# Another order of the hand-written step list behind the attention: row norms, weight halves, modulation rows and feed-forward heads

## Chip, cores, metric

The kernel runs on one core of one Trainium2 chip. The metric is the time of one execution on the device in microseconds (us). The core's engines work side by side, each through a queue of its own in order: PE (TensorE) multiplies and transposes, ACT (ScalarE) and DVE (VectorE) work elementwise and read the results of PE, POOL (GpSimd) works elementwise as well, SP (SyncE) starts most DMA transfers. An engine waits at an instruction until what it reads is written, and everything behind that instruction in its queue waits with it.

## The reference

Two layers of a diffusion backbone over 512 latent tokens and 256 context tokens of width 1024, batch 1. Layer 0 mixes tokens by windowed attention, layer 1 by a gMLP; behind each stands a SwiGLU FFN.

```python
for i in range(DEPTH):
    sh_ml, sc_ml, g_ml, sh_fl, sc_fl, g_fl = jnp.split(silu(c) @ ada_w[i] + ada_b[i], 6, axis=-1)
    h_l = modulate(rmsnorm(x, norm_g[i, 0]), sh_ml, sc_ml)          # h * (1 + scale) + shift
    if kind == 0:
        y_l, y_c = window_sink_mixer(h_l, h_c, ...)
    elif kind == 1:                                                 # gMLP
        z = gelu(h_l @ w_in + b_in)
        u, v = split(z)
        v = layernorm(v, ln_g, ln_b)                                # in chunks of 128 tokens
        y_l = (u * (einsum('gpq,bnqgc->bnpgc', w_s, v) + b_s)) @ w_o
    x = x + g_ml * rmsnorm(y_l, norm_g[i, 1])
    h = modulate(rmsnorm(x, norm_g[i, 2]), sh_fl, sc_fl)
    gate, up = jnp.split(h @ ffn_w_in[i], 2, axis=-1)
    x = x + g_fl * rmsnorm((silu(gate) * up) @ ffn_w_out[i], norm_g[i, 3])
```

## The kernel before

Products are computed in split precision: each float32 operand becomes a high half (`high`, L216, a cast on ACT, L217) and a low half (`low`, L219, a subtraction on DVE, L224), and each product is three matmuls: high by high, high by low, low by high (L273 to L275, L281). Weights come in units through a stream: `wfetch_u` starts the load of unit u on SP, `whigh_u_h` and `wlow_u_h` make the halves of its half h.

The 512 tokens are four row tiles of 128. Behind each mixer's and each FFN's last product, a `Chain` object for each tile t does what the lines of the reference between two products say. Its steps, with their engines, are: `square_y` (ACT), `gain_y` (DVE, L1150), `rstd_y` (DVE, then a power on POOL, L254), `add_x` (DVE, L1154), `square_x` (ACT), `gain_x` (POOL, L1166), `rstd_x` (DVE, POOL), `shift_x_z` (DVE, L1170) for the halves z, `turn_z` (four PE transposes, L1177), `turned_hi_z` (ACT) and `turned_lo_z` (DVE), which write the operand H of the next product. In the step list they are `c0square_y`, `c1turn_0` and so on; "#2" and "#3" mark the second and third use of a name. `c2merge` and `c3merge` add a part of the attention's out-projection that was computed earlier.

Four groups of steps are drawn into the change's reach:

- The last two units of the attention's out-projection (`work_2_t`, `work_3_t`: 12 matmuls of 512 columns each), made by `down`, with the four chains and the heads of FFN 0. A head is the first hidden tile's product for one row tile: `f0head_t_0` and `f0head_t_1` are 12 matmuls each, `f0head_t_2` is Silu on ACT (L1328), its product with the other half on DVE (L1329), and, for t over 0, the PE transposes (L1338) of tile t − 1 and their copy on DVE (L1339). Beside them stand the preparations of the FFN's later products, which are done in a fast-multiplication scheme with sums and differences of quarters: `f0first_half` (ACT), `f0sum_a_*` (DVE, L1378), `f0sum_high_*` and `f0sum_low_*` (the halves of these sums), `f0diff_2_*` (POOL, L1409), `f0part_high_*` and `f0part_low_*` (halves of weight quarters). The FFN's own products (L1449) come behind.
- The last units of FFN 0's second product (`work_9_t`, `work_10_t`), with the chains and the first two units of the gMLP's v (`<lambda>_t_n`).
- The gMLP: `v_part`, the layer norm of v (`v0add` to `v3bias`), `u_part`, `mixed_g` (L1882), and two modulation rows, each made from eight chunks (`m2fetch_chunk_k` on SP, `m2add_chunk_k` on DVE, L383), a fold of its halves by a DMA that POOL starts (`m2fold`, L397), and `m2mirror`, `m2stack`, `m2total`, `m2done`; `m4...` likewise.
- The gMLP's out-projection with the chains and the heads of FFN 1 (`f1...`), as in the first group.

What sets the order is one long text, `ORDER` (from L41): the names of all steps in the sequence in which they are to be issued. The code first collects steps with `at(time, step, ...)`, which makes a name and looks up its rank in that text; a step whose name isn't there goes behind all others by its planned time. `run_plan` then sorts what was collected and issues it:

```python
def run_plan():
    for _, _, key, step, args in sorted(plan, key=lambda e: e[:2]):
        step(*args)
    plan.clear()
```

So ranks count only among the steps of one `run_plan`. The attention has its own ones, and each of the four groups above is one. Where the `run_plan` stands in a `manual_schedule`, as for these groups, each engine's queue has the sequence of the text. The steps of the two FFNs between the groups aren't in the text and go by their planned times.

## Time and profile before

| | us |
|---|---|
| median of 3 runs | 1109.13 (1108.85 to 1111.06) |
| the profiled execution, its span from the first to the last instruction | 1108.2 |
| PE, gaps in the span | 19.9 |
| attention's out-projection, last units | about 250 to 300 of the span |
| FFN 0 | 300 to 593 |
| FFN 0's last units | 593 to 643 |
| gMLP | 643 to 717 |
| gMLP's out-projection | about 717 to 789 |
| FFN 1 | 789 to the end |

The profile is of one execution. The page gives each engine's busy time and its share of the span, the clock that TensorE was granted in 40 slices, and for each engine what ended its waits. The trace can be asked for windows (a row for each stretch: length, then busy time and, in brackets, count of instructions for PE, PE's weight loads, DVE, ACT and POOL, then the granted clock, the DMA share and GB/s), for a timeline of one engine (start, length, line, operation, what it writes and reads, and in square brackets the idle time before it and what ended that), and for a line's groups (count, then shortest, median and longest duration in ns). Neighbouring instructions of one kind share a row of the timeline ("x8"); the row's length reaches from the first start to the last end. Rows of DVE follow each other by less than their length, since the start of one overlaps the end of the one before.

### The profile page before, as it was taken

Reading aid. Unit: us, or ns where it says so; the run is one execution under the profiler, and the core shown is the slowest. Engines: PE = TensorE matmul, PEld = TensorE weight load, DVE = VectorE, ACT = ScalarE, POOL = GpSimd, SP = SyncE. Lnnn points to the kernel's source line nnn. Section 1 sums busy time; section 2 is a strip of 40 time slices with the busy share of each in tenths; the row PEclk is TensorE's granted clock in tenths of the full one; section 3 lists DMA queues with packets and bytes.
Section 4 is the critical chain, followed back from the end, with each engine's and each line's share of the span. In section 5 each row is a group of like instructions: output and inputs, shape, how many; then the busy total and the mean of one; then the engine's idle time right before and its main releaser. Section 6 shows DMA issues by size and latency. Waiting matters only on the chain.

```text
span 1108.2 us, 17883 instructions
## 1 busy us (share of the span) xinstructions
PE 1088.3 (98%) x6974; PEld 954.9 (86%) x6974; DVE 943.8 (85%) x1418; ACT 612.6 (55%) x1060; POOL 255.9 (23%) x276
## 2 busy tenths in 40 slices
PE   7999999999999999999999999999999999999997
...
PEclk9999999999999999999999999999999999999999
...
GB/s 366 266 182 86 136 96 115 77 135 113 109 143 172 224 159 185 171 141 330 225 122 128 68 323 241 205 194 77 70 133 124 132 152 126 126 222 319 158 40 76
DMA packets 48857, 179.15 MB, mean 162 GB/s; under 512 B 4859, under 2 KB 9211, under 8 KB 37637
## 3 DMA queue, kind: packets, MB, share of 16 engines
...
q14 instruction: 31, 0.25, 0.1%
...
## 4 chain that ended last, share of the span: by engine, by line
PE 64%; DVE 6%; POOL 2%; issue 2%; ACT 1%; DMA 1%; POOLq 0%; DVEq 0%; SPq 0%; ACTq 0%
PE f L1449 35%; PE y L1633 13%; PE y L1660 4%; PE v L281 4%; PE y L281 2%; PE u L1869 1%; PE u L1867 1%; PE u L1868 1%; POOL tmp L1166 1%; DVE w_lo L224 1%; DVE tmp L1170 1%; DVE x L1154 1%; PE mix L1882 1%; DMA w_raw<-in_w 1%; DVE a_sum L1378 1%
## 5 line engine op out<-in xcount | busy, mean ns | idle before, releaser
L1449 PE MATMUL f<-H,w_hi 128*128 128x256 f32 x960 | 178.6, 284 | 1.1 <-DVE fc L1460 0.5
L1449 PEld LDWEIGHTS f<-H,w_hi 128*128 128x128 f32 x960 | 149.7, 192 | 2.3 <-DVE fc L1460 1.4
L1449 PE MATMUL f<-H,w_lo 128*128 128x256 f32 x480 | 135.8, 283 | 0.0
L1633 PE MATMUL y<-w_hi,s 128*128 128x512 f32 x448 | 120.1, 389 | 0.0
L1449 PE MATMUL f<-S,w_hi 128*128 128x256 f32 x640 | 118.6, 283 | 0.0
L217 ACT CAST w_hi<-w_raw 128x1024 fp32r<-128x1024 f32 x90 | 94.5, 1053 | 39.9 <-PE y L1633 8.9
L217 ACT CAST w_hi<-T 128x1024 fp32r<-128x1024 f32 x80 | 83.7, 1047 | 52.4 <-PE f L1449 33.7
L1456 ACT COPY fc<-f 128x256 f32<-128x256 f32 x120 | 44.6, 372 | 105.8 <-PE f L1449 102.7
L224 DVE TENSOR_TENSOR w_lo<-w_raw,w_hi 128x1024 fp32r<-128x1024 f32 (+1 forms) x81 | 96.3, 1193 | 6.7 <-ACT w_hi L217 6.7
L1449 PEld LDWEIGHTS f<-S,w_hi 128*128 128x128 f32 x640 | 99.9, 192 | 0.0
L1633 PEld LDWEIGHTS y<-w_hi,s 128*128 128x128 f32 x448 | 84.1, 188 | 17.5
L224 DVE TENSOR_TENSOR w_lo<-T,w_hi 128x1024 fp32r<-128x1024 f32 x80 | 97.3, 1216 | 0.0
L1449 PEld LDWEIGHTS f<-H,w_lo 128*128 128x128 f32 x480 | 92.1, 192 | 0.0
L1449 PE MATMUL f<-S,w_lo 128*128 128x256 f32 x320 | 90.7, 284 | 0.5 <-DVE w_lo L224 0.5
L1621 POOL DMA_DIRECT2D t<-in_w x48 | 42.2, 929 | 186.5 <-PE y L1660 88.4
L383 DVE SCALAR_TENSOR_TENSOR acc<-ada_k,sc,acc 128x1024 f32<-128x1024 f32 x56 | 71.6, 1278 | 10.3 <-DMA ada_k<-in_ada 8.4
L397 POOL DMA_DIRECT2D acc<-acc x8 | 6.9, 866 | 314.2 <-DVE acc L383 310.4
L1633 PE MATMUL y<-w_lo,s 128*128 128x512 f32 x224 | 69.1, 390 | 0.6 <-DVE w_lo L224 0.6
L1449 PE MATMUL f<-H,x 128*128 128x256 f32 x480 | 64.3, 283 | 0.0
L932 POOL TENSOR_SCALAR p<-p,st 128x512 f32<-128x512 f32 (+1 forms) x64 | 53.4, 849 | 44.4 <-DVE st L928 11.7
L281 PE MATMUL y<-w_hi,st 128*128 128x512 f32 x224 | 62.3, 391 | 0.0
L1449 PEld LDWEIGHTS f<-S,w_lo 128*128 128x128 f32 x320 | 61.4, 192 | 0.9 <-DVE w_lo L224 0.9
...
## 6 DMA issues: line engine op xcount, KB each, us to landing
...
```

The costliest lines, as they stand in the source:

```text
L217: nc.scalar.copy(out=hi, in_=src)
L224: (eng or nc.vector).tensor_tensor(out=v(lo), in0=v(src), in1=v(hi).bitcast(F32), op=ALU.subtract)
L281: nc.tensor.matmul(dst, l, w[:, n * 512:(n + 1) * 512], start=first and i == 0, stop=last and i == 2)
L383: nc.vector.scalar_tensor_tensor(out=self.acc, in0=self.raws.pop(k), scalar=sc[:, k:k + 1], in1=self.acc, op0=ALU.mult, op1=ALU.add)
L932: nc.gpsimd.tensor_scalar(out=p, in0=p, scalar1=self.st[:, 12 + j:13 + j], scalar2=1.0, op0=ALU.mult, op1=ALU.mult)
L1154: nc.vector.scalar_tensor_tensor(out=xt, in0=self.tmp[:, c0:c1], scalar=self.r, in1=xt, op0=ALU.mult, op1=ALU.add)
L1166: nc.gpsimd.tensor_tensor(out=self.tmp[:, D:], in0=x[:, self.t, :], in1=self.nxt[0], op=ALU.mult)
L1449: nc.tensor.matmul(dst, l[:, w], r[:, k, :], start=first and k == 0 and j == 0, stop=k == 3 and j == 2, skip_group_check=True)
L1456: nc.scalar.copy(out=self.c[n][:, i * 256:(i + 1) * 256], in_=self.ps[n, 1 if i == 1 else 0])
L1621: nc.gpsimd.dma_start(out=self.tt[:, p * D + 512 * i:p * D + 512 * (i + 1)], in_=a["w"][F2[self.layer] + 1 + 2 * p + i][:, c:c + 512], acc ...
L1633: nc.tensor.matmul(self.bank7(i, j), st[:, c:c + P], w[:, z * 512:(z + 1) * 512], start=i == 1 and p == 0 and l == 0 and z == 0, stop=p == ...
L1660: nc.tensor.matmul(self.y[t][n], st[:, x + t * P:x + (t + 1) * P], parts[h][w][:, n * 512:(n + 1) * 512], start=v == 0 and h == 0 and i == ...
```

## The change

Only the text of `ORDER` is another one; no other line of the program differs. The new text has 1571 names instead of 1575; the four that are gone, `v0norm` to `v3norm`, name no step of the program. The attention's part has `q_first_0_1_6`, `m2fold`, `m2mirror`, `kv_7_5`, `m3stack` at other places relative to steps of other groups, and is else as before. The four groups behind it are ordered anew. Their lists, cut to the parts that the text below speaks of:

```diff
-rows_out_15 wo_part_3_1_3 wo_keep_3_1 store_15_1 store_15_0 work_2_0 whigh_10_0 whigh_10_1 m3stack_<lambda> wlow_10_0
-work_3_0 work_2_1 c0square_y wlow_10_1 work_3_1 c0gain_y c0rstd_y wfetch_11 c0add_x whigh_11_0 m3total_0_slot
-m3total_512_slot c0square_x c1square_y work_2_2 c0gain_x wlow_11_0 m3done_0 c0rstd_x c1gain_y m3done_512 work_3_2
-c1rstd_y c0shift_x_1 c0shift_x_0 c1add_x c0turn_1 c0turn_0 c1square_x c1gain_x c2merge work_2_3 c1rstd_x c2gain_y
-c0turned_hi_1 c2square_y c0turned_hi_0 c2rstd_y whigh_11_1 c0turned_lo_0 c1shift_x_0 c2add_x c1shift_x_1 c2gain_x
-work_3_3 table_Silu c2square_x c1turn_0 c3merge c2rstd_x c1turned_hi_0 c1turned_lo_0 f0first_half_1 f0head_0_0
-c1turn_1 wfetch_12 c3square_y c1turned_hi_1 c0turned_lo_1 wlow_11_1 c3rstd_y c3gain_y c2shift_x_0 f0diff_2_1
...
-c2turned_hi_0 c2turned_lo_0 f0sum_a_S2 f0part_low_2_0 c3shift_x_1 f0head_1_2 c3shift_x_0 f0sum_a_S4 f0head_2_0
-c3turn_0 f0first_half_0#2 c3turn_1 f0head_2_1 c3turned_hi_1 c3turned_hi_0 f0diff_2_3 c3turned_lo_0 c3turned_lo_1
-f0diff_2_2 f0diff_2_4 f0part_high_2_1 f0part_high_2_3 f0sum_a_S3#2 f0sum_a_S1 f0sum_a_S2#2 f0head_2_2 f0sum_a_S4#2
-f0sum_a_S1#2 f0head_3_0 f0sum_high_S4 f0sum_high_S2 f0sum_high_S1 f0head_3_1 wfetch_13 f0part_low_2_2 f0sum_low_S2
-f0head_3_2 f0sum_low_S1 f0sum_high_S3 f0part_low_2_1 f0sum_low_S4 f0part_low_2_3 f0sum_low_S3 work_9_1 whigh_43_0
-work_9_0 work_10_0 wlow_43_0 c0square_y#2 whigh_43_1 c0gain_y#2 wfetch_44 c0rstd_y#2 c0add_x#2 work_9_2 whigh_44_0
-<lambda>_1_2 work_10_1 wlow_43_1 wlow_44_0 <lambda>_2_2 c0square_x#2 c0rstd_x#2 c1square_y#2 c1gain_y#2 c0gain_x#2
-c1rstd_y#2 c0shift_x_0#2 wfetch_45 work_9_3 work_10_2 c2square_y#2 c0shift_x_1#2 c1add_x#2 c2gain_y#2 c1gain_x#2
...
-m2add_chunk_2 v0gelu m2fetch_chunk_5 wlow_47_1 v0mean m2add_chunk_3 v0var v_part_1_(3,) v0gain whigh_48_0
-m2add_chunk_4 m2fetch_chunk_6 v0norm m2add_chunk_5 m2fetch_chunk_7 v_part_2_(2,) v1add v0rstd whigh_48_1 m2add_chunk_6
-u_part_0_0 v1gelu m2add_chunk_7 v0bias v1mean m2fold#2 wlow_48_1 wfetch_49 v1gain m2fetch_gain#2 v_part_3_(3,)
...
-whigh_49_1 v2gelu u_part_1_1 v2mean v3add v2var wfetch_50 gelu_u_0_0 v3gelu gelu_u_0_1 v2gain m4add_chunk_1
-m4fetch_chunk_3 m4fetch_chunk_4 wlow_49_1 v2rstd m4add_chunk_2 v3mean wlow_49_0 v2norm v3var v2bias m4fetch_chunk_5
-wfetch_51 m2done_512#2 v3rstd m4add_chunk_3 m4add_chunk_4 m4fetch_chunk_6 u_part_2_1 v3norm whigh_50_0 v3gain
-u_part_2_0 m4add_chunk_5 m4fetch_chunk_7 gelu_u_1_0 gelu_u_1_1 v3bias m4add_chunk_6 m4add_chunk_7 m4fold#2
-m4fetch_gain#2 mixed_0 wlow_50_0 mixed_6 m4mirror#2 whigh_50_1 mixed_bias_0 mixed_1 whigh_51_0 mixed_u_0 mixed_bias_1
-mixed_5 mixed_3 mixed_u_1 mixed_4 mixed_bias_3 gelu_u_2_0 mixed_2 wlow_50_1 mixed_u_3 m4stack#2 u_part_3_0 whigh_51_1
...
-mixed_u_7 whigh_55_0 work_2_0#2 work_3_0#2 whigh_55_1 c0square_y#3 work_2_1#2 work_3_1#2 wfetch_56 whigh_56_0
-wlow_55_0 whigh_56_1 work_2_2#2 c1square_y#3 wlow_55_1 c0rstd_y#3 c0gain_y#3 c0add_x#3 m3total_0_slot#2
-m3total_512_slot#2 c0gain_x#3 c0square_x#3 wlow_56_0 c0rstd_x#3 m3done_512#2 m3done_0#2 work_3_2#2 c2square_y#3
-c1rstd_y#3 c1gain_y#3 c0shift_x_1#3 c0shift_x_0#3 c1add_x#3 c2gain_y#3 c0turn_1#3 c0turn_0#3 c1gain_x#3 c1square_x#3
-c1rstd_x#3 c2rstd_y#3 wfetch_57 c1shift_x_1#3 c0turned_hi_0#3 work_2_3#2 c1shift_x_0#3 c0turned_hi_1#3 c2add_x#3
...
-c3turned_hi_1#3 f1sum_a_S3 f1part_high_2_1 c2turned_lo_0#3 f1sum_a_S2 c2turned_lo_1#3 f1part_low_2_0 f1sum_a_S3#2
-f1sum_a_S1 c3turned_lo_0#3 f1first_half_1#2 f1sum_a_S2#2 f1sum_a_S4 f1head_1_2 f1head_2_0 f1head_2_1 f1sum_a_S4#2
-f1sum_high_S2 f1diff_2_4 f1sum_a_S1#2 c3turned_lo_1#3 f1part_high_2_3 f1head_2_2 f1sum_high_S4 f1head_3_0 f1sum_low_S4
-f1part_low_2_2 f1head_3_1 f1sum_high_S3 wfetch_58 f1sum_high_S1 f1head_3_2 f1sum_low_S1 f1part_low_2_1 f1sum_low_S2
-f1part_low_2_3 f1sum_low_S3
...
+wo_keep_3_1 store_15_1 store_15_0 m3stack_<lambda> work_2_0 whigh_10_0 whigh_10_1 wfetch_11 m3total_0_slot m3done_0
+m3total_512_slot wlow_10_0 work_3_0 c0square_y c0gain_y c0rstd_y c0add_x c0gain_x whigh_11_0 whigh_11_1 work_2_1
+m3done_512 wlow_10_1 work_3_1 c1gain_y c0square_x c0rstd_x c1square_y c1rstd_y wlow_11_0 c1add_x work_2_2 work_3_2
+c0shift_x_1 c0shift_x_0 c0turn_1 c1square_x c1rstd_x c2merge c1gain_x c2gain_y c2square_y c0turn_0 wlow_11_1
+c0turned_hi_0 work_2_3 c1shift_x_0 work_3_3 c2rstd_y c1shift_x_1 c0turned_lo_0 c0turned_hi_1 c1turn_1 c1turn_0
+c1turned_hi_0 c2add_x c2gain_x c3merge c2square_x f0head_0_0 c1turned_lo_0 c0turned_lo_1 c2rstd_x c2shift_x_1
...
+c3turn_0 f0diff_2_1 f0diff_2_3 f0diff_2_2 c2turned_hi_0 c2turned_lo_0 f0head_2_0 f0diff_2_4 c3shift_x_1 wfetch_13
+f0first_half_1 c3turn_1 f0sum_a_S2 c2turned_hi_1 c2turned_lo_1 f0sum_a_S1 f0first_half_1#2 f0head_2_1 f0part_high_2_0
+f0part_low_2_0 c3turned_hi_0 c3turned_lo_0 f0part_high_2_2 f0part_low_2_2 f0sum_a_S4 f0sum_a_S3#2 f0sum_a_S2#2
+f0sum_a_S4#2 f0part_high_2_1 f0sum_a_S1#2 c3turned_hi_1 f0part_high_2_3 f0sum_high_S4 f0head_1_2 f0sum_high_S1
+f0part_low_2_1 f0sum_high_S2 f0head_3_0 c3turned_lo_1 f0sum_low_S2 f0sum_low_S1 f0head_2_2 f0sum_low_S4 f0head_3_1
+f0sum_high_S3 f0head_3_2 f0part_low_2_3 f0sum_low_S3 table_Silu whigh_43_0 whigh_43_1 wlow_43_1 <lambda>_3_2 wfetch_44
+work_9_1 work_10_1 c1square_y#2 c1gain_y#2 c1rstd_y#2 c1add_x#2 c1gain_x#2 whigh_44_0 whigh_44_1 wlow_43_0 work_9_0
+work_10_0 c0gain_y#2 <lambda>_1_2 c0square_y#2 c0rstd_y#2 c0add_x#2 c0square_x#2 c1square_x#2 work_9_3 wlow_44_0
+c0gain_x#2 <lambda>_2_2 c0rstd_x#2 c0shift_x_1#2 work_9_2 work_10_2 c2square_y#2 c0turn_1#2 c0turned_hi_1#2
...
+v_part_1_(2,) v_part_1_(3,) row_in_1 m2add_chunk_2 m4fetch_chunk_0 m2fetch_chunk_5 v_part_2_(2,) m2fetch_chunk_6 v0add
+v_part_2_(3,) m2add_chunk_3 m2add_chunk_4 whigh_47_1 m2add_chunk_5 v_part_3_(2,) v_part_3_(3,) wlow_47_0 wfetch_48 v1add
+v1gelu m2fetch_chunk_7 v0gelu m2add_chunk_6 v0mean m4fetch_chunk_1 m2add_chunk_7 wlow_47_1 m2fold#2 row_in_2 v0var
...
+wlow_49_1 v3mean m4fetch_chunk_5 m4fetch_chunk_7 wlow_48_1 u_part_1_0 v2add v2gelu m4add_chunk_0 m4add_chunk_1 v3var
+m2total_0_slot wfetch_50 wlow_49_0 m4add_chunk_2 m4add_chunk_3 v2mean v2gain bias_in v3rstd v3gain v3bias ws_in
+gelu_u_0_0 m4fetch_gain#2 m4add_chunk_4 m4add_chunk_5 u_part_2_0 m4fetch_chunk_6 m4add_chunk_6 m4add_chunk_7 m4fold#2
+v2var v2rstd gelu_u_2_0 wfetch_51 whigh_50_0 whigh_50_1 m2total_512_slot v2bias wlow_50_0 u_part_2_1 gelu_u_2_1
+whigh_51_0 gelu_u_0_1 whigh_51_1 m2fetch_gain#2 m2done_512#2 wlow_51_1 u_part_1_1 mixed_1 m2done_0#2 mixed_2
+mixed_bias_1 mixed_u_1 wlow_50_1 mixed_5 mixed_3 gelu_u_1_0 mixed_0 gelu_u_1_1 mixed_4 mixed_bias_5 mixed_u_5
...
+mixed_u_6 gelu_u_3_1 mixed_7 mixed_bias_7 mixed_u_7 work_2_0#2 work_2_1#2 whigh_55_0 wlow_55_0 work_3_0#2 c0gain_y#3
+c0square_y#3 c0rstd_y#3 c0add_x#3 c0gain_x#3 work_3_1#2 c1gain_y#3 c1square_y#3 c1rstd_y#3 m3total_0_slot#2 c0square_x#3
+c0rstd_x#3 whigh_55_1 wlow_55_1 m3total_512_slot#2 wfetch_56 m3done_512#2 work_2_2#2 m3done_0#2 c0shift_x_0#3 work_3_2#2
+c0shift_x_1#3 whigh_56_0 c0turn_1#3 whigh_56_1 wfetch_57 c2square_y#3 c0turn_0#3 c1add_x#3 c1square_x#3 c1gain_x#3
+wlow_56_0 c2gain_y#3 work_2_3#2 c0turned_hi_0#3 c1rstd_x#3 c0turned_lo_0#3 f1first_half_1 c1shift_x_1#3 c2rstd_y#3
...
+f1sum_a_S3 f1sum_a_S2 f1diff_2_1 c3turn_0#3 c3shift_x_1#3 c2turned_hi_0#3 c2turned_lo_0#3 f1sum_a_S1 f1part_high_2_2
+c2turned_hi_1#3 c2turned_lo_1#3 f1first_half_0#2 f1diff_2_3 f1head_1_1 f1head_1_2 f1diff_2_2 c3turn_1#3 f1sum_a_S4
+c3turned_hi_1#3 c3turned_lo_1#3 f1diff_2_4 c3turned_hi_0#3 f1head_2_0 f1part_low_2_2 f1head_2_1 c3turned_lo_0#3
+f1sum_a_S3#2 f1sum_a_S2#2 f1part_high_2_3 f1sum_a_S1#2 f1sum_a_S4#2 f1part_low_2_3 f1sum_high_S1 f1sum_low_S1
+f1sum_high_S4 f1head_3_0 f1sum_low_S4 f1sum_high_S3 f1sum_low_S3 f1part_high_2_1 f1part_low_2_1 f1head_2_2 f1head_3_1
+f1sum_high_S2 f1sum_low_S2 f1head_3_2 table_Silu#2
```

Split into queues, the end of the first group reads on DVE and PE, before and after:

```
DVE before: ... f0head_1_2 c3shift_x_0 f0sum_a_S4 c3turned_lo_0 c3turned_lo_1 f0sum_a_S3#2 f0sum_a_S1 f0sum_a_S2#2 f0head_2_2
            f0sum_a_S4#2 f0sum_a_S1#2 f0part_low_2_2 f0sum_low_S2 f0head_3_2 f0sum_low_S1 ...
DVE after:  ... f0sum_a_S1 f0part_low_2_0 c3turned_lo_0 f0part_low_2_2 f0sum_a_S4 f0sum_a_S3#2 f0sum_a_S2#2 f0sum_a_S4#2
            f0sum_a_S1#2 f0head_1_2 f0part_low_2_1 c3turned_lo_1 f0sum_low_S2 f0sum_low_S1 f0head_2_2 f0sum_low_S4 f0head_3_2 ...
PE before:  ... f0head_1_1 f0head_1_2 f0head_2_0 c3turn_0 c3turn_1 f0head_2_1 f0head_2_2 f0head_3_0 f0head_3_1 f0head_3_2
PE after:   ... f0head_1_1 c3turn_0 f0head_2_0 c3turn_1 f0head_2_1 f0head_1_2 f0head_3_0 f0head_2_2 f0head_3_1 f0head_3_2
```

The end of the fourth group:

```
DVE before: ... f1sum_a_S1#2 c3turned_lo_1#3 f1head_2_2 f1sum_low_S4 f1part_low_2_2 f1head_3_2 f1sum_low_S1 f1part_low_2_1
            f1sum_low_S2 f1part_low_2_3 f1sum_low_S3
DVE after:  ... f1sum_a_S4#2 f1part_low_2_3 f1sum_low_S1 f1sum_low_S4 f1sum_low_S3 f1part_low_2_1 f1head_2_2 f1sum_low_S2 f1head_3_2
PE before:  ... f1head_2_1 f1head_2_2 f1head_3_0 f1head_3_1 f1head_3_2
PE after:   ... f1head_2_1 f1head_3_0 f1head_2_2 f1head_3_1 f1head_3_2
```

More of the change, by code (lines that the diff above doesn't have):

```diff
@@ L121 @@
[L121 to L124 removed]
+norm_in_4_1 turn_in_4_1 ada0_rows_out_3 modulated_low_1 modulate0_ctx_2 kv_1_2 kv_1_4 kv_1_5 turned_in_0_1 turned_in_4_1
@@ L155 @@
-c3turn_0 f0first_half_0#2 c3turn_1 f0head_2_1 c3turned_hi_1 c3turned_hi_0 f0diff_2_3 c3turned_lo_0 c3turned_lo_1
-f0diff_2_2 f0diff_2_4 f0part_high_2_1 f0part_high_2_3 f0sum_a_S3#2 f0sum_a_S1 f0sum_a_S2#2 f0head_2_2 f0sum_a_S4#2
-f0sum_a_S1#2 f0head_3_0 f0sum_high_S4 f0sum_high_S2 f0sum_high_S1 f0head_3_1 wfetch_13 f0part_low_2_2 f0sum_low_S2
-f0head_3_2 f0sum_low_S1 f0sum_high_S3 f0part_low_2_1 f0sum_low_S4 f0part_low_2_3 f0sum_low_S3 work_9_1 whigh_43_0
-work_9_0 work_10_0 wlow_43_0 c0square_y#2 whigh_43_1 c0gain_y#2 wfetch_44 c0rstd_y#2 c0add_x#2 work_9_2 whigh_44_0
@@ L195 @@
[L195 to L199 removed]
+rows_out_11 store_11_0 turned_12_2 bound_14_2 exp_14_2 bound_14_3 turn_12_3 wo_part_2_1_2 m3add_5 wo_part_2_1_3 exp_14_3
@@ L200 @@
+f1sum_high_S4 f1head_3_0 f1sum_low_S4 f1sum_high_S3 f1sum_low_S3 f1part_high_2_1 f1part_low_2_1 f1head_2_2 f1head_3_1
+f1sum_high_S2 f1sum_low_S2 f1head_3_2 table_Silu#2
 """.split()
```

233 lines of the change are left out of this document (115 added, 118 removed).

## Prediction

> **What bounds the kernel now.** I read the page first: its busy line, its clock row, then the waits of PE, then the windows of the stages whose order changes.
>
> ```profile
> span 1108.2 us, 17883 instructions
> PE 1088.3 (98%) x6974; PEld 954.9 (86%) x6974; DVE 943.8 (85%) x1418; ACT 612.6 (55%) x1060; POOL 255.9 (23%) x276
> ...
> PEclk9999999999999999999999999999999999999999
> ```
> ```profile
> PE hT L1177 <- DVE tmp L1170: 2.5, 5, 1.1
> ...
> PE f L1449 <- DVE w_lo L224: 0.5, 1, 0.5
> ```
> ```profile
> core 0: us, PE busy (x) PEld busy (x) DVE busy (x) ACT busy (x) POOL busy (x), PEclk, DMA share, GB/s
> 250.00:300.00 50.00, 49.44 (x237) 40.37 (x236) 44.93 (x62) 31.30 (x55) 30.78 (x21) 1.00 0.27 90
> 300.00:350.00 50.00, 49.52 (x412) 49.23 (x411) 50.00 (x68) 26.68 (x45) 0.00 (x0) 1.00 0.50 169
> 593.00:643.00 50.00, 48.63 (x228) 39.55 (x227) 37.15 (x52) 23.41 (x42) 15.77 (x13) 1.00 0.39 134
> 643.00:717.00 74.00, 74.00 (x360) 62.44 (x359) 60.56 (x73) 31.58 (x44) 8.68 (x8) 1.00 0.73 250
> 738.00:790.00 52.00, 51.13 (x243) 40.99 (x242) 44.13 (x64) 34.18 (x61) 31.05 (x21) 1.00 0.25 82
> ...
> 850.00:950.00 100.00, 100.00 (x836) 100.00 (x835) 87.98 (x125) 52.47 (x90) 0.00 (x0) 1.00 0.38 136
> ```
>
> PE is busy 98% of the span at full clock, so only its gaps can be won. The changed stages are four: the last half of the attention's out-projection (250 to 300, its end reaching to 304), the last units of FFN 0 (593 to 643), the gMLP (643 to 717) and its out-projection (738 to 790). Their PE gaps are 0.56 + 0.48 + 1.37 + 0 + 0.87 = 3.28 us, most of it in transposes that wait for `shift_x` (L1177 for L1170). This is **all the change can win**; what it can lose has no such bound, for inside these stages every engine takes its instructions in the order of the list. DVE beside them is 74 to 100% busy, so a step that goes later in DVE's queue soon makes PE wait. PE's instructions are the same before and after, so I walk DVE's, ACT's and POOL's new queues and look where PE reaches a step before its operand.
>
> **The change, part by part.** It adds and removes no work: of the names that go, four (`v0norm` to `v3norm`) name no step. Ranks count only within one `run_plan`, so the attention's rows, which move only against other plans' rows, cost and win nothing. The Silu table load comes to lie ahead of the first Silu, where ACT waits for PE's head anyway: nothing.
>
> *Attention out-projection.* First its front, then its tail.
>
> ```profile
> 265.06 1.42 DVE L1170 SCALAR_TENSOR_TENSOR tmp<-tmp,rx,row 128x512 f32<-128x512 f32 x2 [0.41 <-POOL rx L254]
> 266.39 1.28 DVE L1154 SCALAR_TENSOR_TENSOR x<-tmp,ry,x 128x1024 f32<-128x1024 f32 x1
> ```
> ```profile
> 292.39 1.29 DVE L224 TENSOR_TENSOR H<-hT,H 128x512 fp32r<-128x512 f32 x2 [0.67 <-ACT H L217]
> ...
> 295.39 0.41 DVE L1329 TENSOR_TENSOR silu_a<-fa,silu_a 128x256 f32<-128x256 f32 x1
> 295.73 0.41 DVE L1339 COPY act<-fat 128x256 f32<-128x256 f32 x1
> ...
> 298.37 1.21 DVE L224 TENSOR_TENSOR w_lo<-w_raw,w_hi 128x1024 fp32r<-128x1024 f32 x1
> 299.50 1.21 DVE L224 TENSOR_TENSOR S<-a_sum,S 128x1024 fp32r<-128x1024 f32 x1
> ```
> ```profile
> 296.77 1.05 ACT L217 CAST s<-a_sum 128x1024 fp32r<-128x1024 f32 x1 [2.24 <-DVE a_sum L1378]
> ...
> 299.79 0.38 ACT L1328 ACTIVATE silu_a<-fa 128x256 f32<-128x256 f32 x1
> ```
> ```profile
> 266.96 1.03 PE L1177 MATMUL hT<-ident,tmp 128*128 128x128 f32 x8
> ...
> 299.53 0.38 PE L1338 MATMUL fat<-ident,silu_a 128*128 128x128 f32 x2
> 299.67 1.67 PE L1449 MATMUL f<-H,x 128*128 128x256 f32 x12
> ```
>
> Before, the two `c0shift_x` were done at 266.5 and PE turned at 266.96. Now a low half (`wlow_11_0`) and `c1add_x` (1.28) stand ahead of them; the low half fits into gaps, `c1add_x` doesn't: PE waits about 0.6 here, and some tenths at later turns. Those waits lie ahead of the tail and don't add to it, because **DVE sets the tail**. One 1024-wide low half costs 299.50 − 298.37 = 1.13. Ahead of the product of tile 1 (`f0head_1_2`) now stands all that DVE had done by 298.37, less `c3turned_lo_1` (0.60, half of the row at 292.39) and two products with copies (0.67 each), plus `f0part_low_2_2` (1.13): 297.6. ACT is later still: its Silu of tile 1 is behind `f0sum_high_S4`, whose source is written one sum (0.6) before that point: 297.0 + 1.05 + 0.38 = 298.4. So the product ends at 298.7, and PE, whose transposes of it now come after `f0head_3_0`, waits (it is there near 297, by 299.53 less one head of 2.72). Then, in DVE's queue: copy 0.33, `f0part_low_2_1` 1.13, `c3turned_lo_1` 0.60: 300.8. Only then can PE start `f0head_3_1` (before: H complete at 293.7). One head is (299.53 − 293.86)/2, less transposes, 2.72, so the first product of FFN 0 starts at 300.8 + 2.72 + 0.14 = 303.6 where it was 299.67: +3.9; +3.1 if ACT isn't late.
>
> ```profile
> 300.00:590.00 290.00, 288.38 (x2059) 272.45 (x2058) 269.43 (x359) 160.38 (x256) 24.87 (x28) 1.00 0.62 186
> ```
>
> The wait of 0.48 at `w_lo` goes; of the other 1.62 − 0.48 = 1.1 us of PE gaps in the FFN behind I count half as taking up the delay. **Net +2.9**; ends +1.2 (ACT in time, all gaps absorb, one sum fewer is slowed) and +4.3.
>
> How much the sums on DVE slow under POOL's `diff` is unknown in the new order; two rows bound it:
>
> ```profile
> L1378 DVE TENSOR_TENSOR a_sum<-a_sum x8: 675/1062/1785, 290.0 to 783.0; 128x512 f32<-128x512 f32 x8
> L1378 DVE TENSOR_TENSOR a_sum<-a_sum,hT x4: 678/679/686, 282.5 to 778.0; 128x512 f32<-128x512 f32 x4
> ```
>
> The form with both operands in SBUF takes 0.68 to 1.79, the one with an operand in PSUM always 0.68. In this stage four such sums stand near the tail: so 1.1 us more or less if one more or one fewer is hit; the ends above hold that. [...]
>
> *Last units of FFN 0.* `work_10_1` goes from fifth to second, so it starts near 596.2 and needs the second low half of its unit after 8 matmuls of 0.227, near 598.0.
>
> ```profile
> 598.35 1.22 DVE L224 TENSOR_TENSOR w_lo<-w_raw,w_hi 128x1024 fp32r<-128x1024 f32 x1
> ```
> ```profile
> 617.65 1.32 PE L1177 MATMUL hT<-ident,tmp 128*128 128x128 f32 x8 [1.08 <-DVE tmp L1170]
> ...
> 620.10 3.26 PE L281 MATMUL v<-w_lent,H 128*128 128x512 f32 x13 [0.20 <-DVE H L224]
> ```
>
> That half is written at 599.57: a wait of 1.6. In return tile 1's norm starts 5 us sooner, and this stage's gaps of 1.37, the 1.08 at 617.65 above all, go. New small waits at tile 2's turn (about 0.3) give **+0.5**; ends −1.0 and +1.5.
>
> *gMLP.*
>
> ```profile
> 685.16 1.28 DVE L1857 SCALAR_TENSOR_TENSOR v<-vtmp,rv,row 128x1024 f32<-128x1024 f32 x1
> ...
> 691.92 1.28 DVE L1857 SCALAR_TENSOR_TENSOR v<-vtmp,rv,row 128x1024 f32<-128x1024 f32 x1
> 694.06 2.61 DVE L383 SCALAR_TENSOR_TENSOR acc<-ada_k,sc,acc 128x1024 f32<-128x1024 f32 x2 [0.86 <-DMA ada_k<-in_ada]
> ```
> ```profile
> 697.08 0.83 POOL L397 DMA_DIRECT2D acc<-acc  x1 [0.72 <-DVE acc L383]
> ```
> ```profile
> 697.83 5.41 PE L1882 MATMUL mix<-ws,v 128*128 128x128 f32 x47
> ```
>
> The `v_part` and `whigh` moves keep 3 us or more of slack. But `v2rstd` and `v2bias` (were at 685) move behind the last four `m4add_chunk` on DVE, and on POOL behind `m4fold`. SP too sends chunk 6 after the bias and gain rows. If the adds end as before at 696.6, then come fold 0.83 (at 697.08), the power 0.55 to 1.5 and `v2bias` 1.28: 699.7 to 700.7, where PE wants to mix at 697.8: a wait of 1.9 to 2.9. If the loads come 2.5 us sooner, as `m4fetch_chunk_0` and others are now sent earlier, there is none. I take **+1.3**, ends 0 and +2.9.
>
> *gMLP out-projection.*
>
> ```profile
> 756.61 1.32 PE L1177 MATMUL hT<-ident,tmp 128*128 128x128 f32 x8 [0.64 <-DVE tmp L1170]
> ...
> 789.15 1.68 PE L1449 MATMUL f<-H,x 128*128 128x256 f32 x12
> ```
> ```profile
> 785.33 0.41 DVE L1329 TENSOR_TENSOR silu_a<-fa,silu_a 128x256 f32<-128x256 f32 x1
> ...
> 785.99 1.21 DVE L224 TENSOR_TENSOR s<-a_sum,s 128x1024 fp32r<-128x1024 f32 x1
> 787.12 2.31 DVE L224 TENSOR_TENSOR w_lo<-w_raw,w_hi 128x1024 fp32r<-128x1024 f32 x1
> ```
>
> The front turns later by about 0.6 as before, again ahead of a tail that DVE sets. The product of tile 2 (`f1head_2_2`, 785.33) falls behind six low halves that followed it: `f1part_low_2_2`, `_2_3`, `_2_1`, `f1sum_low_S1`, `S4`, `S3`: 6 × 1.13 = 6.8, so it ends at 785.33 + 6.8 + 0.33 = 792.5. PE's `f1head_3_2` transposes it directly ahead of FFN 1 and is ready near 790: it waits 2.5, and the first product starts at 792.6 instead of 789.15: +3.5. Tile 3's product comes one low half later and holds the next transposes about 0.3. FFN 1 gives nothing back (PE 100.00 of 100). **Net +3.8**; ends +2.4 (DVE's gaps are filled) and +5.2 (one more low half at 2.31).
>
> **Sum:** 2.9 + 0.5 + 1.3 + 3.8 = +8.5, of which I take off 1 us, as each of my walks holds DVE to its old gaps, which a changed queue may fill: **+7.5**. On the profiled execution's span of 1108.2 this is 1115.7; on the median of the runs, 1109.13, which is 0.9 above that span, 1116.6.
>
> **The rivals.**
> - *Faster, 1106*: the tails are covered, and the 3.28 us of gaps go. It is decided at two places: product of tile 1 by 297, product of tile 2 by 790. For it: the waits on L1170 are real, and tile 1 of FFN 0 starts sooner. Against: the six low halves. 6 in 100.
> - *No change, 1109*: F2 wins 1, FFN 0 absorbs its 1.6 of gaps, and the last tail costs under 2; or the queues' order hardly matters while PE is 98% busy. Against: FFN 1 has no gap. 7 in 100.
> - *Only the last tail, 1113* (+3.8): DVE in the first one catches up with the 0.67 gap at 292.39 and the mix isn't late. 13 in 100.
> - *A clock drop, 1119*: the two waits of the first tail (about 1.7 each, 0.14 of work between) halve PE's clock for as long, and 3.4 us at half speed lose 1.7, in a second tail 1.0 more. The longest gap here that lies amid matmuls is 1.08 at 617.65, with a granted clock of 1.00 in its window. 5 in 100. [...]
> - My forecast, all four terms near their values: 69 in 100.
>
> A measurement of this kernel can tell about 0.2% (2.2 us) from no change. Faster than that 0.06, within it 0.07, slower 0.87. The range, 1110.5 to 1121, leaves out the two first rivals and the case of all terms at their upper ends (+13.9, 1123).
>
> **What would show it.** In the waits of PE: L1338 on `silu_a` L1329, about 1.7 before FFN 0 and 2.5 before FFN 1; L273 to L275 on `H` L224, about 1.7, in the first tail; L1882 on `v` L1857, 1 to 3; a matmul of FFN 0's unit 10 on `w_lo`, 1.6; the wait of 1.08 at L1177 gone. The first `f<-H,x` of FFN 0 near 303, that of FFN 1 near 796. Wrong, if these transposes don't wait, or if DVE's queue isn't in list order.

## The result and the profile after

| | median us | ratio to before, 95% interval |
|---|---|---|
| before | 1110.02 (1108.85 to 1111.06) | |
| after (profiled span 1150.7) | 1152.66 (1149.11 to 1153.17) | 1.0376 [1.0358, 1.0393] |

The new order costs 42.6 us; +7.5 was forecast, and the time lies far above the range. The direction and some of the places were right, the sizes not. All lines of code in the changed kernel are three lower: L1177 is L1174, L1338 is L1335, L1449 is L1446, L224 is L221. The page of after:

```profile
span 1150.7 us, 17890 instructions
PE 1100.9 (96%) x6974; PEld 962.2 (84%) x6974; DVE 953.4 (83%) x1418; ACT 613.0 (53%) x1060; POOL 255.5 (22%) x276
...
PEclk9999999999899999999999999999899999999999
```

The same 6974 matmuls keep PE busy 1100.9 − 1088.3 = 12.6 us longer, and its idle time grows from 19.9 to 1150.7 − 1100.9 = 49.8, by 29.9: together 42.5, the whole loss. Most of the first part is clock: 27.3 us of the trace lie at a granted clock of 0.50 (302.64 to 312.88, 742.96 to 749.79, 787.33 to 790.75 and 828.29 to 835.12), and PE is busy for 22.7 of them, of which up to half, 11.4, is added by it (an estimate). The second is waiting; slow matmuls also fill time in which PE would else have waited, so the two don't part cleanly into causes. What PE waited for (total, times, longest):

```profile
PE fat L1335 <- DVE silu_a L1326: 8.6, 2, 5.4
PE hT L1174 <- DVE tmp L1167: 7.2, 8, 2.1
PE mix L1879 <- DVE v L1854: 3.1, 1, 3.1
PE y L278 <- DVE row L418: 3.0, 1, 3.0
PE ada_ps L407 <- DVE acc_st L221: 2.9, 1, 2.9
...
PE y L1657 <- DVE w_lo L221: 1.4, 1, 1.4
```

The first, third and last are the waits that the prediction named (the tails, the mix, the low half of unit 10); the second it named as small (0.6 us and some tenths). The fourth and the fifth, in the modulation rows, it didn't name. The windows of the stages, PE first, the clock behind POOL:

```profile
250.00:311.60 61.60, 53.15 (x236) 41.97 (x235) 51.10 (x65) 32.54 (x55) 31.00 (x21) 0.93 0.30 101
...
605.00:655.00 50.00, 47.24 (x219) 37.82 (x218) 36.80 (x51) 25.25 (x44) 17.10 (x13) 1.00 0.33 111
655.00:738.00 83.00, 75.40 (x360) 62.61 (x359) 63.94 (x76) 28.40 (x40) 7.68 (x8) 1.00 0.70 241
738.00:829.50 91.50, 78.08 (x337) 61.94 (x336) 69.16 (x87) 39.74 (x69) 29.38 (x21) 0.94 0.29 97
850.00:950.00 100.00, 100.00 (x836) 100.00 (x835) 87.00 (x124) 52.14 (x90) 0.00 (x0) 1.00 0.38 132
```

The middle of the FFN is as before, 100 of 100; nearly all of the loss is in the four groups. The first tail shows both parts at once, in the timeline of PE and then in the windows:

```profile
304.86 0.69 PE L1335 MATMUL fat<-ident,silu_a 128*128 128x128 f32 x2 [5.44 <-DVE silu_a L1326]
...
308.37 0.63 PE L272 MATMUL fa<-w_lent,H 128*128 128x512 f32 x1
...
311.64 1.20 PE L1446 MATMUL f<-H,x 128*128 128x256 f32 x4
```
```profile
300.00:304.00 4.00, 0.00 (x0) 0.00 (x0) 2.74 (x5) 2.41 (x4) 2.18 (x2) 0.83 0.91 367
304.00:308.00 4.00, 2.62 (x7) 1.71 (x8) 3.62 (x6) 3.44 (x6) 0.00 (x0) 0.50 0.02 7
308.00:312.00 4.00, 4.00 (x13) 3.13 (x11) 2.93 (x4) 0.41 (x2) 0.00 (x0) 0.50 0.00 0
```

PE waits 5.44 for the product of tile 1, then works for about 8 us at a granted clock of 0.50, where a head matmul takes 0.63 instead of 0.39. FFN 0 begins at 311.64 (before: 299.67; forecast: 303.6).

### The profile page after: what moved, and what is told of

Its sections match the earlier page's. It is cut to its first block, busy times and chain, and to the rows that moved or that the text cites. A ratio compares the mean times of both kernels' runs of the same rounds, so it can differ in the third digit from the quotient of the medians.

```text
span 1150.7 us, 17890 instructions
## 1 busy us (share of the span) xinstructions
PE 1100.9 (96%) x6974; PEld 962.2 (84%) x6974; DVE 953.4 (83%) x1418; ACT 613.0 (53%) x1060; POOL 255.5 (22%) x276
## 4 chain that ended last, share of the span: by engine, by line
PE 53%; DVE 10%; issue 5%; DMA 4%; POOL 2%; ACT 1%; DVEq 0%; POOLq 0%; SPq 0%; ACTq 0%
PE f L1446 34%; PE y L1630 10%; PE y L1657 3%; PE y L278 3%; DMA ada_k<-in_ada 2%; PE v L278 2%; DVE w_lo L221 2%; DMA acc<-acc 1%; DVE acc L380 1%; DVE tmp L1167 1%; DVE a_sum L1375 1%; POOL tmp L1163 1%; DVE H L221 1%; DVE x L1151 1%; POOL ry L251 0%
## 5 line engine op out<-in xcount | busy, mean ns | idle before, releaser
L1446 PE MATMUL f<-H,w_hi 128*128 128x256 f32 x960 | 179.6, 285 | 1.1 <-DVE fc L1457 0.5
L1446 PEld LDWEIGHTS f<-H,w_hi 128*128 128x128 f32 x960 | 150.7, 193 | 2.2 <-DVE fc L1457 1.4
L1446 PE MATMUL f<-H,w_lo 128*128 128x256 f32 x480 | 136.3, 284 | 0.0
L1446 PE MATMUL f<-S,w_hi 128*128 128x256 f32 x640 | 118.5, 283 | 0.0
L221 DVE TENSOR_TENSOR w_lo<-w_raw,w_hi 128x1024 fp32r<-128x1024 f32 (+1 forms) x81 | 96.4, 1195 | 18.7 <-ACT w_hi L214 18.7
L221 DVE TENSOR_TENSOR w_lo<-T,w_hi 128x1024 fp32r<-128x1024 f32 x80 | 97.5, 1219 | 6.5 <-ACT w_hi L214 6.5
L1446 PEld LDWEIGHTS f<-S,w_hi 128*128 128x128 f32 x640 | 100.0, 192 | 0.0
L1446 PEld LDWEIGHTS f<-H,w_lo 128*128 128x128 f32 x480 | 92.7, 193 | 0.0
L1446 PE MATMUL f<-S,w_lo 128*128 128x256 f32 x320 | 90.5, 283 | 0.0
L1618 POOL DMA_DIRECT2D t<-in_w x48 | 42.6, 944 | 185.1 <-PE y L1657 88.7
L380 DVE SCALAR_TENSOR_TENSOR acc<-ada_k,sc,acc 128x1024 f32<-128x1024 f32 x56 | 71.7, 1281 | 8.0 <-DMA ada_k<-in_ada 7.7
L278 PE MATMUL y<-w_hi,st 128*128 128x512 f32 x224 | 64.5, 403 | 3.3 <-DVE row L418 3.0
L1446 PE MATMUL f<-H,x 128*128 128x256 f32 x480 | 66.0, 288 | 0.0
L1446 PEld LDWEIGHTS f<-H,x 128*128 128x128 f32 x480 | 62.3, 197 | 0.1
## 6 DMA issues: line engine op xcount, KB each, us to landing
ada<-in_ada SPq DMA_DIRECT2D x8, 1024.0 KB, 11.4
```

The costliest lines, as they stand in the source:

```text
L221: (eng or nc.vector).tensor_tensor(out=v(lo), in0=v(src), in1=v(hi).bitcast(F32), op=ALU.subtract)
L278: nc.tensor.matmul(dst, l, w[:, n * 512:(n + 1) * 512], start=first and i == 0, stop=last and i == 2)
L380: nc.vector.scalar_tensor_tensor(out=self.acc, in0=self.raws.pop(k), scalar=sc[:, k:k + 1], in1=self.acc, op0=ALU.mult, op1=ALU.add)
L1446: nc.tensor.matmul(dst, l[:, w], r[:, k, :], start=first and k == 0 and j == 0, stop=k == 3 and j == 2, skip_group_check=True)
L1618: nc.gpsimd.dma_start(out=self.tt[:, p * D + 512 * i:p * D + 512 * (i + 1)], in_=a["w"][F2[self.layer] + 1 + 2 * p + i][:, c:c + 512], acc ...
```

## The experiments

All rest on one idea: `ORDER` is put together from old and new lists; only *wo_fill* has other code too. Times are medians beside runs of before on the same chip.

**One group alone.** Each kernel takes one group's list from the diff above (those that begin with `work_2_0`, with `whigh_43_0`, at the gMLP, and with `work_2_0#2`) and leaves the other three old. Theory A: each group costs by itself what its marks lost in the trace; theory B: it costs the prediction's term, and the rest comes of their sequence.

> New order in the attention's out-projection alone. Theory A (the loss sits in the four groups one by one, as the trace of the changed kernel shows it): FFN 0 started 11.5 us later there and took 0.3 less, so +11 us here. Theory B (the prediction's walk is right for each group, and the rest comes from groups acting on each other): +3. Under A PE's wait of 5.4 us ahead of the transposes of tile 1 is there again, with a granted clock of 0.5 behind it.

> New order in FFN 0's last units alone. Theory A: +2.5 us (waits of 1.45 on the weight half and 0.8 at the first turn, less the old waits). Theory B: +0.5.

> New order in the gMLP alone. Theory A: about +14 us: +7.7 inside the group, and behind it the wait of 3.0 us on a bank that the modulation row's step holds, with 8 us at about half clock. Theory B: +1.3.

> New order in the gMLP's out-projection alone. Theory A: about +13 us: +10.7 inside the group and +2.2 in FFN 1's first products at half clock. Theory B: +3.8. The four runs of this call add up to about 41 under A, to under 15 under B.

| kernel | us | ratio | over before | term forecast |
|---|---|---|---|---|
| only_wo | 1120.27 | 1.0091 [1.0074, 1.0109] | 10.8 | 2.9 |
| only_f2 | 1113.58 | 1.0035 [1.0017, 1.0052] | 4.1 | 0.5 |
| only_gm | 1123.46 | 1.0121 [1.0103, 1.0138] | 14.0 | 1.3 |
| only_go | 1121.12 | 1.0103 [1.0084, 1.0123] | 11.6 | 3.8 |

The sum is 40.5 of 42.6, so most of the cost adds up, and every term was too small. The intervals reach about 1.8 us to either side: a difference of 1 or 2 us between two of these kernels says nothing by itself. Where the cost lies is seen in the traces, one execution each, by the time from the first product of a stage to that of the next:

| from, to | before | after | one group alone |
|---|---|---|---|
| attention's out-projection (`work_2`), FFN 0 | 60.4 | 71.9 | 71.7 (only_wo) |
| FFN 0's second product, gMLP's v | 113.8 | 115.0 | 115.0 (only_f2) |
| v, mix | 79.1 | 81.8 | 80.4 (only_gm) |
| mix, gMLP's out-projection | 18.4 | 25.0 | 25.0 (only_gm) |
| gMLP's out-projection, FFN 1 | 72.9 | 91.1 | 77.7 (only_gm), 82.5 (only_go) |
| FFN 1's first product, its second | 201.0 | 203.2 | 201.9 (only_go) |

The groups aren't wholly apart. Of only_gm's 14.0 us, 4.8 lie behind its group, in the out-projection whose list is old there. In that stage after loses 18.2, where the two groups alone lose 4.8 and 9.6, so up to some 4 us come of their sequence. And of only_f2's 4.1 just 2.0 lie behind its first changed step (1.3 up to v, 0.8 from there to the mix); most of the rest, 1.8, lies ahead of `work_2`, where it is like before, and so is scatter.

**The first tail, step by step.** Four kernels with only the first group new, each with one suspect put back: the Silu and product of tile 1; the same with tile 3's second half; PE's gap filled with 24 idle products into an unused part of the bank (a bank is a part of PSUM, to which this kernel has PE write its results); and the order in which ACT and DVE read one PSUM bank (high halves ahead of sums, squares ahead of gains).

```diff
 wo_silu
-... f0sum_high_S4 f0head_1_2 f0sum_high_S1 ...
+... c3turn_1 f0head_1_2 f0sum_a_S2 ...
 wo_tail, as wo_silu and
+... c3turned_lo_0 c3turned_hi_1 c3turned_lo_1 f0part_high_2_2 ...
 wo_fill, in the head's transposes
+for _ in range(24 if (self.layer, t) == (0, 1) else 0):
+    nc.tensor.matmul(pt[:, 384:512], ident, ident, start=True, stop=True)
 wo_readers
+... c2turned_hi_0 f0sum_a_S3 ... c2turned_hi_1 f0sum_a_S2 ...
+... f0part_high_2_1 c3turned_hi_1 f0sum_a_S2#2 ... c0square_x c1square_y c1gain_y ...
```

> The first group's new order (it cost 10.8 us alone), with one step put back: the Silu step of tile 1 (its cast on ACT, its product on DVE, the transposes of tile 0) directly behind PE's last turn. Theory 'one late step' (the Silu of tile 1 alone holds PE): the wait of 5.4 us goes and with it the half clock, +2 to +4 us remain. Theory 'late queue' (everything in DVE's tail is late, and PE's next operand, the low half of tile 3's second half, comes no sooner than before less what was taken out of its way): the wait only moves on to the head that reads H, 4 to 6 us long, and +8 to +10 remain.

> As the run before, and also tile 3's second half is split right behind its first half, ahead of the sums. Under both theories the wait at the end goes now: +2 to +4 us remain (the waits at the turns, 0.8 + 0.7 + 1.0 before, stay) and the granted clock stays at 1.0 behind it. If +7 or more remain, the tail was not what cost the time.

> The first group's new order, untouched, with 24 idle matmuls of 128 columns on PE ahead of the transposes that wait 5.4 us. They write a part of a bank that nobody reads and end before the operand comes. Theory 'clock' (a gap this long halves PE's clock for some us and this costs 2.5 to 3 us): 7.5 to 8.5 of the 10.8 us remain, the granted clock is 1.0 behind it. Rival (the slow matmuls lie in time that PE would have waited anyway): 10.8 remain.

> The first group's new order; each engine has exactly the same queue as there. Only the place in the list between engines differs: ACT's reads of a bank (the high halves of tiles 2 and 3, the square of tile 1) are listed ahead of DVE's reads of the same bank (the sums, the gain). Theory 'readers' (two engines that read one bank are made to take turns in list order, and this is what ACT's 10.4 us of waits for sums come from): those waits go, the product of tile 1 comes 1 to 2 us sooner, and 8.5 to 10 us remain of 10.8. Rival (the list acts by the queues alone): 10.8, and ACT's waits stay.

| kernel | us | ratio | over before |
|---|---|---|---|
| wo_silu | 1119.65 | 1.0084 [1.0066, 1.0101] | 9.4 |
| wo_tail | 1118.75 | 1.0078 [1.0063, 1.0093] | 8.5 |
| wo_fill | 1117.51 | 1.0068 [1.0053, 1.0083] | 7.3 |
| wo_readers | 1120.93 | 1.0101 [1.0082, 1.0121] | 10.7 |

*wo_fill* does what was said: DVE's product comes hardly sooner (its transposes start at 304.75, in only_wo at 304.94), yet 10.8 − 7.3 = 3.5 us return. In its timeline of PE the gap is full, and the head behind it runs at 0.39 to 0.40, at a granted clock of 1.00:

```profile
299.16 5.52 PE L1335 MATMUL fat<-ident 128*128 128x128 f32 x48
304.75 0.44 PE L1337 MATMUL fat<-ident,silu_a 128*128 128x128 f32 x2
```

So clock is a part of the group's 10.8 us, but not all of the 3.5. The intervals of the two kernels overlap, and in the traces the stage up to FFN 0 is 1.8 us shorter than in only_wo (69.9 to 71.7); the rest lies in the gMLP's out-projection (70.6 to 72.8), which both leave old. In only_wo PE works 5.45 us at half clock (304.09 to 310.91), which can cost half of that, 2.7, at most (an estimate). About 2 us is what the runs bear out. Putting steps back gave little, since the next operand was as late. The waits of *wo_tail* in the same place, rows of its timeline of PE:

```profile
296.12 0.50 PE L270 MATMUL fa<-w_lent,H 128*128 128x512 f32 x1 [1.73 <-ACT H L214]
...
309.93 0.69 PE L1335 MATMUL fat<-ident,silu_a 128*128 128x128 f32 x2 [4.56 <-DVE silu_a L1326]
```

Now the product of tile 2 is late instead of that of tile 1: 2 to 4 us were expected to be left, 8.5 were. *wo_readers* clears the waits that I suspected most. ACT's waits in only_wo, then in wo_readers:

```profile
ACT H L214 <- DVE a_sum L1375: 10.4, 3, 5.5
```
```profile
ACT H L214 <- PE hT L1174: 7.1, 2, 5.2
ACT s L214 <- DVE a_sum L1375: 6.5, 1, 6.5
```

The high halves no longer wait for sums (another cast of ACT's waits 6.5 for one instead), and the time is the same: by what is measured, ACT's 10.4 us weren't what held PE.

**The last two groups, step by step.** Only that group new, and one suspect put back: the product of tile 2 in the last tail; the readers' order there; the last steps of v's third row; the last step of the second modulation row, whose bank the next product needs.

```diff
 go_prod
+... f1sum_a_S4#2 f1head_2_2 f1part_low_2_3 ...
 go_readers
+... c0square_y#3 c0gain_y#3 ... c1square_y#3 c1gain_y#3 ... c2turned_hi_0#3 f1sum_a_S3 ...
+... f1part_high_2_2 c2turned_hi_1#3 f1sum_a_S2 ...
 gm_v2
+... v2gain v2var v2rstd v2bias bias_in ...
 gm_done
+... m4total_0_slot m4done_0#2 mixed_bias_4 ...
```

> The fourth group's new order (it cost 11.6 us alone), with one step put back: the Silu step of tile 2 ahead of the five low halves. The prediction's walk priced this at 3.5 us without a change of clock. With the clock (0.5 behind the wait of 3.2 us) it is 3.2 + about 2.5: 5.5 to 6.5 us remain of 11.6. By the walk alone 8 remain.

> The fourth group's new order, each engine's queue the same; in the list ACT's squares of tiles 0 and 1 stand ahead of DVE's gains of the same banks, and ACT's high halves of tile 2 ahead of DVE's sums. Theory 'readers': ACT's squares start 0.6 to 1.3 us sooner, the first turn's wait falls from about 2 to 1 or less, ACT's wait of 5.8 us at tile 2's high half goes; 8 to 10.5 us remain. Rival (queues alone): 11.6.

> The gMLP's new order (it cost 14.0 us alone), with the variance, power and bias of v's tile 2 ahead of the last four chunk additions and of the fold on POOL. The wait of 3.2 us at the mix goes; what follows (the bank that is held, half clock) stays: 10 to 11.5 remain. If the mix then waits for something else, 13 to 14.

> The gMLP's new order, with the last step of the modulation row (which frees the bank that the out-projection's first tile takes next) directly behind its PE step. Theory: the wait of 2.9 us goes, and with it 3 to 4 us of half clock: 7 to 9 us remain of 14.0. Rival (the wait only names that step, another step holds PE): 13 or more.

They stay at 12.2 (1.0114 [1.0099, 1.0129]), 11.5 (1.0104 [1.0087, 1.0121]), 13.0 (1.0121 [1.0103, 1.0139]) and 13.6 us (1.0124 [1.0109, 1.0139]): none returns anything that can be measured. The expectations had 5.5 to 6.5 (8 without the clock), 8 to 10.5, 10 to 11.5 and 7 to 9 us left; only the rivals of the second and the last (11.6; 13 or more), and for the third "13 to 14", fit. In go_prod the stage is 2.1 us shorter than in only_go (80.4 to 82.5), but FFN 1's first product then takes 4.0 longer (205.9 to 201.9). In gm_v2 the wait of the mix is gone from PE's list, and another stands there:

```profile
PE ada_ps L407 <- DVE acc_st L221: 4.9, 1, 4.9
PE y L278 <- DVE row L418: 2.0, 1, 2.0
```

**Halves of a group.** If no single step holds PE, the question is which kind of step does. The first and the last group are cut in two: in *chain* only the names `c0...` to `c3...` (the row norms) have their new places among the old others, in *rest* everything else has. The gMLP is cut likewise: in *gm_vu* the modulation rows are old and all else new. *gm_adds* takes the whole new list and moves the last two additions of the second row and its fold behind the last step of the first (`m2done_0#2`). Cut to the first tail:

```diff
 wo_chain, against before
-f0part_low_2_0 c3shift_x_1 f0head_1_2 c3shift_x_0 f0sum_a_S4 f0head_2_0 c3turn_0
+c3shift_x_0 c3turn_0 c2turned_hi_0 c2turned_lo_0 f0sum_a_S2 c3shift_x_1 ... f0head_1_2 f0sum_a_S4
 wo_rest, against before
-f0sum_a_S2 f0part_low_2_0 c3shift_x_1 f0head_1_2 c3shift_x_0
+c3shift_x_0 f0head_2_0 f0sum_a_S2 ... f0part_high_2_3 f0sum_high_S4 f0head_1_2 c3turned_lo_1
 gm_adds, against only_gm
-m4fetch_chunk_6 m4add_chunk_6 m4add_chunk_7 m4fold#2 v2var
+m4fetch_chunk_6 v2var ... m2done_0#2 m4add_chunk_6 m4add_chunk_7 m4fold#2 mixed_2
```

> Only the stage of the output projection is changed, and in it only the steps of the row norms (squares, gains, adds, shifts, transposes and the halves of the transposed tiles) take their new places; weight halves, the FFN's sums, parts, sum halves and products keep the old ones. If it is the new places of the sums, parts and products that hold the first FFN matmul (theory preparation), the row norms alone cost what the last transposes lost, about 3 us: 1112 to 1114. If it is the row norms themselves (theory norms), nearly all of the stage's 10.8 us is there: 1118 to 1121.

> The other half of the same stage: weight halves, sums, parts, sum halves and products in their new places, the row norms in the old ones. Theory preparation: 7 to 10 us over the kernel before, 1117 to 1120. Theory norms: 0 to 3 us, 1110 to 1113. If both halves cost little (under 3 us each), neither alone holds it, and the delay is made where a late tile meets a late product.

> Only the stage of the gated output is changed, and in it only the steps of the row norms take their new places. Theory norms (tile 3's late transposes and the gains at the stage's front hold it): 8 to 12 us over the kernel before, 1118 to 1122. Theory preparation (sums, parts and products): 2 to 5 us, 1112 to 1115.

> The other half of that stage: weight halves, sums, parts, sum halves and products in their new places, the row norms in the old ones. Theory preparation: 6 to 10 us, 1116 to 1120. Theory norms: 0 to 3 us, 1110 to 1113.

> Only the stage of the gated MLP is changed, and in it the steps of the modulation rows (fetches, additions, folds, stacks, sums) keep their old places; v, u, the mix and the weight halves take their new ones. If it is the late fetches of the row's chunks that put VectorE behind (theory late chunks: it waits 12.9 us for them in the stage alone, against 8.4 before), nearly all of the 14 us goes: 1110 to 1114. If the new places of v, u, the mix and the weight halves do it (theory weights), it stays: 1119 to 1124.

> The stage of the gated MLP alone in its new order, with the last two additions of the second row and its fold moved behind the last step of the first row, so that the last row of v and three weight halves no longer stand behind the chunk for which VectorE waited 4.96 us. Theory late chunks: that wait and the 3.2 us that the mix waited for v go, 3 to 6 us come back: 1117 to 1120. Theory weights: no gain, 1122 to 1124.

| kernel | us | ratio | over before |
|---|---|---|---|
| wo_chain | 1114.55 | 1.0042 [1.0026, 1.0058] | 5.3 |
| wo_rest | 1116.87 | 1.0067 [1.0050, 1.0084] | 7.6 |
| go_chain | 1119.41 | 1.0090 [1.0074, 1.0106] | 10.1 |
| go_rest | 1117.76 | 1.0075 [1.0059, 1.0091] | 8.5 |
| gm_vu | 1123.63 | 1.0118 [1.0103, 1.0133] | 13.3 |
| gm_adds | 1125.12 | 1.0136 [1.0120, 1.0153] | 14.8 |

In the first group the preparation costs more, as expected, though the intervals overlap; the row norms alone cost 5.3, where about 3 was said. In the last group the halves cost 18.6 where the whole costs 11.6: each by itself makes PE wait, in another place, and the costs overlap. PE's waits in that stage, go_chain and then go_rest:

```profile
PE hT L1174 <- DVE rx L248: 5.1, 1, 5.1
PE hT L1174 <- DVE tmp L1167: 2.7, 1, 2.7
```
```profile
PE fat L1335 <- DVE silu_a L1326: 4.6, 1, 4.6
PE hT L1174 <- DVE tmp L1167: 1.2, 3, 0.8
```

In the gMLP "late chunks" falls: with the rows in their old places DVE waits only 7.0 us for chunks (12.9 in only_gm, 8.4 before), and 13.3 us stay. What its five kernels share is seen in windows of 80 us from the first product of v, which before end as the mix begins (before, only_gm, gm_v2, gm_done, gm_vu, gm_adds):

```profile
618.72:698.72 80.00, 79.80 (x366) 65.99 (x364) 62.45 (x78) 33.14 (x47) 16.09 (x13) 1.00 0.64 226
```
```profile
618.69:698.69 80.00, 79.19 (x356) 64.66 (x355) 58.39 (x73) 30.50 (x44) 12.98 (x12) 1.00 0.62 216
```
```profile
619.68:699.68 80.00, 79.38 (x358) 65.00 (x357) 59.86 (x75) 30.63 (x44) 13.57 (x13) 1.00 0.61 212
```
```profile
620.29:700.29 80.00, 79.40 (x359) 65.24 (x358) 59.37 (x73) 30.57 (x45) 13.68 (x12) 1.00 0.61 217
```
```profile
620.97:700.97 80.00, 78.81 (x356) 64.71 (x355) 60.16 (x76) 32.35 (x46) 14.22 (x12) 1.00 0.64 224
```
```profile
619.39:699.39 80.00, 79.44 (x359) 65.07 (x358) 59.38 (x74) 30.53 (x44) 13.26 (x12) 1.00 0.62 217
```

PE has lost at most 1.0 us by then (79.80 to 78.81), but DVE (third) has done 2.3 to 4.1 us less than its 62.45. Behind this point it has no room to catch up: in only_gm it is busy 7.95 of 8 us from 716 to 724 and 7.62 in the next 8, and PE waits now at a row, now at a low half, whichever stands last. That this debt of DVE is the cause is a reading that fits all five; a kernel that pays off the debt alone was not run, and which of v, u, the mix and the weight halves makes it stays open. The last group speaks against DVE's busy time alone as a measure: in 72.9 us from its first product DVE is busy 61.5 us before, and 62.3 in go_readers and 63.0 in go_rest, which cost 11.5 and 8.5 all the same. The cause in the gMLP isn't shown.

## Why the prediction was wrong, by its steps

- **Its failed step** is the one on which all walks stand: that DVE and ACT come to a tail at their old times, so that only the names newly ahead of a product are to be priced ("DVE sets the tail"). By it the product of tile 1 would end at 298.7. In only_wo DVE begins it at 304.46 (a row of ACT's timeline, then one of DVE's):

```profile
304.04 0.39 ACT L1325 ACTIVATE silu_a<-fa 128x256 f32<-128x256 f32 x1
```
```profile
304.46 0.42 DVE L1326 TENSOR_TENSOR silu_a<-fa,silu_a 128x256 f32<-128x256 f32 x1 [1.50 <-ACT silu_a L1325]
```

  The names were right and the times were not. The windows from `work_2`'s first product to the point that the walk starts from in before, then to that product in only_wo (DVE is third); the same for the last tail and the product of tile 2, before and only_go:

```profile
239.24:298.37 59.13, 58.57 (x274) 47.93 (x273) 47.62 (x67) 35.35 (x59) 33.18 (x25) 1.00 0.27 90
```
```profile
239.63:304.46 64.83, 57.23 (x265) 46.02 (x263) 48.97 (x63) 34.53 (x57) 33.81 (x25) 1.00 0.30 106
```
```profile
716.26:785.33 69.07, 68.20 (x315) 55.06 (x314) 57.71 (x80) 36.72 (x66) 27.21 (x19) 1.00 0.36 122
```
```profile
716.62:798.25 81.63, 73.66 (x331) 59.22 (x329) 69.39 (x86) 39.01 (x69) 29.43 (x21) 0.98 0.34 115
```

  In the first tail 63 instructions of DVE lie ahead of the product, as walked: 67, less `c3turned_lo_1` and two products with their copies, plus one low half. By the walk they take 46.8 us; they take 48.97, and DVE is idle for 15.9 us instead of 11.5. So DVE begins the product 2.2 + 4.3 = 6.5 us after the point at which the walk has it free (297.6), and 5.7 after the one at which the walk has ACT's Silu done (298.4). In the last tail the six low halves make 80 into 86, as walked; they take 69.4 us instead of 64.5, and the gaps grow by 0.9: 5.8 us later, nearly all by slower instructions. Of the first tail's new gaps 1.5 is the wait for ACT's Silu in the row above (0.8 by the walk); most of the others are longer waits for steps of the row norms on POOL and ACT. DVE's waits from 260 to 312, before and then only_wo (total, times, longest):

```profile
DVE tmp L1170 <- POOL rx L254: 0.9, 2, 0.4
DVE x L1154 <- POOL ry L254: 0.7, 1, 0.7
```
```profile
DVE tmp L1167 <- POOL rx L251: 1.7, 2, 1.1
DVE x L1151 <- POOL ry L251: 1.6, 3, 0.7
DVE ry L250 <- ACT junk L241: 1.3, 1, 1.3
```

- **"Those waits lie ahead of the tail and don't add to it"** is refuted by wo_chain: row norms in their new places, with preparation and products in their old ones, cost 5.3 us, and FFN 0 begins 4.2 us later behind the stage's start (64.7 to 60.4). PE waits 0.92 and 0.50 at turns of the first tiles and 1.65 at a turn of tile 3, whose steps are new there too.
- **The 1 us taken off**, for gaps that a changed queue may fill, had the wrong sign: DVE's gaps grew, by 4.3 and 0.9 us ahead of the two products.
- **The clock** was priced at nothing in the sum and at 1.7 us for the first tail in the rival "a clock drop". The rival's mechanism happened, with one gap of 5.4 in place of two of 1.7, and cost about 2 there; it had a chance of 5 in 100, and the sum had no term for it. Two waits close together did it too: in wo_silu PE waits 1.44 and 1.63, with two matmuls between (up to 303.54 and 305.93); the granted clock is 0.73 from 304 to 308 and 0.84 from 308 to 312, and head matmuls take 0.63 from 306.52 on. So the clock should have had a term even with the forecast's waits.
- **Out-projection of the attention:** +2.9 said, 10.8 measured. It waited at the place named, 5.4 instead of 1.7; the half clock adds about 2, and smaller waits, at the transposes above all, the rest. The 1.1 us for sums that are slower beside POOL were too narrow a bound: see the last section.
- **FFN 0's last units:** +0.5 said, 4.1 measured, of which the trace shows 2.0 behind the first changed step. The wait at the low half is 1.4 (1.6 said), but the gap at the transposes, counted as won, is there again (0.9 of 1.1).
- **gMLP:** +1.3 said, 14.0 measured. The mix waits 3.1 for v (upper end 2.9). Not seen were the rows and low halves behind it, where most of the cost is: 1.3 us up to the mix, 6.5 from there to the out-projection, 4.8 behind, with 10.2 us of only_gm's trace at half clock (704.22 to 707.63, 728.11 to 734.94). gm_v2 shows that taking that one wait away is worth nothing. Which step of the walk failed here stays open.
- **Its out-projection:** +3.8 said, 11.6 measured. The last transposes wait 3.2 (2.5 said); the front (row norms, go_chain) was held to be free and alone costs 10.1.
- Right were the sign, that PE does the same work, that most of the cost is a sum over the groups, and that FFN 1 gives nothing back.
